# mLSTM head norm: the scale moved from VectorE into ScalarE's output gate

## The chip, the cores and the metric

The kernel runs on one core of a Trainium2 chip. The metric is the device time of the program in microseconds (us). TensorE is PE in the profile (PEld its weight loads), VectorE is DVE, ScalarE is ACT, GpSimd is POOL, SyncE is SP.

## The reference

One layer of a bidirectional encoder, in fp32, with D = 1024, on a prompt of 2048 positions and a sample of 256:

```python
def encoder_layer(x, ...):
    p = rmsnorm(x, norm1_w) @ w_in
    mq, mk, mv, mo, gates, aq, ak, av = split(p)
    m_out = mlstm_mixer(mq, mk, mv, mo, gates, b_gates, mh_norm_w)     # 8 heads of 64
    a_out = attention_mixer(aq, ak, av, q_norm_w, k_norm_w)            # 8 heads, 2 kv heads
    x = x + concatenate([m_out, a_out]) @ w_out
    u = centred_dwconv(rmsnorm(x, norm2_w) @ w_up, conv_w, conv_b)
    a, g = split(u)
    return x + (silu(g) * a) @ w_down                                  # then a final rmsnorm

def mlstm_mixer(...):
    ...
    h = h_f + h_b                                                      # forward and backward scans
    h = h * lax.rsqrt(jnp.mean(h * h, axis=-1, keepdims=True) + EPS)   # over the 64 of a head
    h = h * mh_norm_w
    return sigmoid(mo) * h
```

The change concerns the last three lines of `mlstm_mixer`.

## The kernel before

The 2304 tokens are worked as 18 tiles of 128 (NT) or 9 blocks of 256 (NB). fp32 products are made of three passes on a high and a low part of each operand ("split": ScalarE rounds, VectorE subtracts). The program has these stages, by the profile's clock: projections for attention and gates (to about 200 us); attention and mLSTM side by side (to 1450); the rest of attention beside phase_c, the output projection (to 1740); the rest of phase_c (to 1850); the up projection with its convolution; the down projection and the final norm.

`run_both` (L1562) steps two generators, `attention` (L458) and `mlstm` (L673), by estimated costs, and once the mLSTM is done it gives attention's steps out beside those of phase_c. The order that each engine runs is not this order of the code: the tile framework's scheduler puts the instructions of every engine in order from its own timeline of estimated costs, with priorities (`high_priority(offset=MPRI)` around the mLSTM's output steps). So a change of a few instructions can move many others.

The mLSTM works its 8 heads as 4 pairs, p = 0 to 3 (LASTP = 3). For each pair it has weights, projection (`proj`, `projT`), state updates (`upd`, `recur`), and then the output steps over the 18 tiles: `out_a` loads the decay matrix dm by a DMA of POOL's queue, masks it on POOL and takes Exp on ScalarE (L828), and for pairs 0 to 2 loads the gate tile `ogr` for two tiles of 128 (L833, POOL's queue); `out_b` and `out_c` make h; `out_d` follows DLAG = 6 steps later. The stored gate is the tanh form: sigmoid(mo) = 0.5 (1 + og), the half is in mhw.

In `out_c`, h is in the tile `hh` (128 tokens x 2 heads x 64) after L869. ScalarE squares each head with a sum along the row (L872), `rstd_of` makes r = (mean + eps)^-0.5 on POOL with two small operations (L97, L98), VectorE multiplies hh by r (L874) and, in pairs 0 to 2, makes (og + 1) * hh (L876). In `out_d` TensorE transposes hh (L881); pairs 0 to 2 scale it by mhw on ScalarE (L884); the last pair, whose gate is kept in transposed layout, multiplies by it on VectorE (L886). The result goes to mix_d in memory.

Attention takes scores (px, maximum over them on VectorE, L561), scores again with the maximum taken off (ps, L582 and L583), Exp on ScalarE (pe, L586), a rounded copy on ScalarE (xx, L587), the low part on VectorE (L588), and three products (pv, L599 to L601). At the end of a query block ScalarE copies the result out (L609), VectorE divides (L614, L615), and it goes to mix_d (L621).

phase_c (L945) takes for a block of 256 tokens eight chunks of mix_d (cmx: load L965, high part on ScalarE L966, low part on VectorE L967; chunk 7 is attention's last), 48 matmuls for each of four output slices z (`po`, L989), then adds the residual on VectorE (cx, L996, which frees the PSUM buffer), squares it on ScalarE (L999), sums (L1003), and at the end takes the norm (`rstd_bc`: PE L128, DVE L134, POOL L143 or, for the last block, ScalarE's square root and DVE L138 to L141, PE L145), and scales on VectorE (L1014). The blocks go in the order 0, 1, 2, 3, 4, 5, 8, 6, 7. In block 6, z = 0 and 1 are worked together and chunk 7 is taken last. Then the up projection loads and splits its first operands (n, rn, nt: L1077, L1092, L1096) and weights (L1110, L1125), and multiplies (pa, pb, pc at L1152).

Of the kernel before, what the change touches and what calls it, by code (L numbers as in the profile page):

```python
# [11 lines left out]
AF = mybir.ActivationFunctionType  # L12
ALU = mybir.AluOpType
# [4 lines left out]
P = 128  # L18
# [75 lines left out]
def rstd_of(g, pool, ms, n, name):  # L94
    nc = g.nc
    r = pool.tile([P, n], F32, tag="rstd", name=name)
    nc.gpsimd.tensor_scalar(r, ms, EPS, None, ALU.add)  # L97
    nc.gpsimd.tensor_tensor(r, r, g.mhalf[:, 0:n], ALU.pow)  # L98
    return r
# [573 lines left out]
def mlstm(g, tc, s1, sp, sw, sn, pj_, pm):  # L673


    nc = g.nc
# [177 lines left out]
    def out_c(s, i, o):  # L854
        nm = f"{s.p}_{i}"
        s1 = o.s1
        pN = pm.tile([P, 2, 2, 65], F32, tag="m", name="mN" + nm)
        for d in range(2):
            for h in range(2):
                nc.tensor.matmul(pN[:, d, h, :], o.dm[:, d, h, :], s.va[i // 2][:, i % 2, h, :], start=True, stop=True)  # L860
        nc.vector.tensor_tensor(s1, pN, s1, ALU.add)
        dn = sp.tile([P, 2, 2], F32, tag="dn", name="dn" + nm, bufs=4)
        nc.vector.scalar_tensor_tensor(dn, s1[:, :, :, 64], -1.0, s1[:, :, :, 64], ALU.mult, ALU.max)
        nc.vector.tensor_tensor(dn, dn, tm[:, i, 3, :, s.hs], ALU.max)
        nc.vector.reciprocal(dn, dn)
        nc.vector.tensor_tensor(s1[:, :, :, 0:64], s1[:, :, :, 0:64],
                                dn.unsqueeze(3).to_broadcast([P, 2, 2, 64]), ALU.mult)
        hh = o.hh = sp.tile([P, 2, 64], F32, tag="hh", name="hh" + nm, bufs=DLAG)
        nc.vector.tensor_tensor(hh, s1[:, 0, :, 0:64], s1[:, 1, :, 0:64], ALU.add)  # L869
        ms = sp.tile([P, 2], F32, tag="mms", name="mms" + nm, bufs=4)  # L870
        for h in range(2):
            nc.scalar.activation(s1[:, 0, h, 0:64], hh[:, h, :], AF.Square, scale=0.125, accum_out=ms[:, h:h + 1])  # L872
        r = rstd_of(g, sp, ms, 2, "mr" + nm)
        nc.vector.tensor_tensor(hh, hh, r.unsqueeze(2).to_broadcast([P, 2, 64]), ALU.mult)  # L874
        if s.p < LASTP:
            nc.vector.scalar_tensor_tensor(hh, o.og.rearrange("p (h d) -> p h d", h=2), 1.0, hh, ALU.add, ALU.mult)  # L876

    def out_d(s, i, o):
        nm = f"{s.p}_{i}"
# [25 lines left out]
    def out_steps(s):  # L905
        os_ = {}
        s.og = {}
        for i in range(NT + DLAG):
            if s.p == LASTP and i % 2 == 0 and i < NT:
                proj_qo(s, i // 2)  # L910
            if DLAG <= i:
                with tc.high_priority(offset=MPRI):
                    out_d(s, i - DLAG, os_.pop(i - DLAG))
            if 2 <= i < NT + 2:
                with tc.high_priority(offset=MPRI):
                    out_c(s, i - 2, os_[i - 2])
            if 1 <= i < NT + 1:
                with tc.high_priority(offset=MPRI):
                    out_b(s, i - 1, os_[i - 1])
            if i < NT:  # L920
                os_[i] = out_a(s, i)
            yield (2.7 if s.p < LASTP else OW3) if i < NT else 1
# [728 lines left out]
```

## Time and profile before

| | before |
|---|---|
| median of 3 runs | 3327.17 us (3326.01 to 3334.67) |
| profiled execution | 3327.39 us, span 3325.7 us |
| busy: PE, DVE, ACT, POOL | 97%, 73%, 60%, 16% |
| mean granted TensorE clock | 0.992 |

The times are of whole executions; the profile is of one further execution, its span is from the first to the last instruction. Lines such as L874 are those of the kernel before. In the changed kernel every line from L877 on has a number higher by 5, so L989 there is L994, and L996 there is L1001.

### The profile page before, as it was taken

How to read it: one execution, taken by the hardware profiler on the slowest of the kernel's cores; microseconds unless marked ns; L12 is line 12 of the kernel's file. 1: busy time of each engine (PE TensorE's matmuls, PEld its weight loads, DVE VectorE, ACT ScalarE, POOL GpSimd, SP SyncE). 2: the span in 40 equal slices, each digit the busy share in tenths (PEclk: the TensorE clock that was granted, in tenths of full speed). 3: DMA queues.
4: the chain of work that ended last, by engine and by line, in shares of the span. 5: the costliest groups of instructions: out<-in, count | busy, mean ns of one | idle time of the engine just before them, and what ended most of it. 6: DMA issues, size and time to landing. Idle time of an engine off the chain costs nothing.

```text
span 3325.7 us, 53327 instructions
## 1 busy us (share of the span) xinstructions
PE 3238.2 (97%) x19488; PEld 3017.3 (91%) x19488; DVE 2429.5 (73%) x3768; ACT 2002.8 (60%) x3765; POOL 519.0 (16%) x916
## 2 busy tenths in 40 slices
PE   8989999999999999999999899999999999999998
PEld 7878888888888878878889899999999999999998
DVE  7855676676657778786665899998888888666664
ACT  5646666666675676665552655666666667554543
POOL 4551033222232322210000000000000000010101
PEclk9999999999999999999999899999999999999999
DMA  9973333332335433533227666668676557967663
GB/s 348 319 207 108 113 113 102 110 108 94 109 114 177 131 110 120 162 100 107 85 89 266 230 240 211 231 231 273 205 266 235 202 199 252 318 229 269 216 238 127
DMA packets 364301, 612.31 MB, mean 184 GB/s; under 512 B 31605, under 2 KB 220455, under 8 KB 364039
## 3 DMA queue, kind: packets, MB, share of 16 engines
q1 hardware_dynamic: 330727, 563.14, 50.4%
q0 software_dynamic: 11856, 33.96, 3.7%
q10 hardware_dynamic: 21456, 11.80, 1.2%
q8 instruction: 154, 2.52, 0.3%
q14 instruction: 108, 0.88, 0.1%
HBM read 444.85 MB, written 163.93 MB: 183 GB/s over the span
## 4 chain that ended last, share of the span: by engine, by line
PE 58%; issue 3%; DVE 2%; DMA 2%; ACT 2%; POOL 1%; SPq 0%; POOLq 0%; DVEq 0%; ACTq 0%
PE pa L1152 17%; PE pc L1152 8%; PE pf L1416 7%; PE po L989 5%; PE pb L1152 4%; PE ph L1416 4%; PE pg L1416 2%; PE ps L582 1%; PE mj L745 1%; PE ps L583 1%; PE pv L599 1%; PE pv L601 1%; PE pv L600 1%; PE px L559 1%; PE mv L745 1%
## 5 line engine op out<-in xcount | busy, mean ns | idle before, releaser
L588 DVE TENSOR_TENSOR xx<-pe,xx 128x1024 fp32r<-128x1024 f32 x260 | 318.8, 1227 | 128.1 <-ACT xx L587 126.5
L561 DVE TENSOR_REDUCE mx<-px 128x1 f32<-128x1024 f32 x256 | 310.8, 1217 | 100.2 <-PE px L559 99.1
L586 ACT ACTIVATE pe<-ps 128x1024 f32<-128x1024 f32 x260 | 266.4, 1025 | 171.0 <-PE ps L583 164.2
L587 ACT ACTIVATE xx<-pe 128x1024 fp32r<-128x1024 f32 x260 | 274.9, 1058 | 5.0
L1369 POOL TENSOR_TENSOR sq<-sq,sq 128x384 f32<-128x384 f32 x38 | 48.8, 1284 | 1377.9 <-ACT sq L1365 1294.9
L989 PEld LDWEIGHTS po<-cmx,wo 128*128 128x128 f32 x1728 | 227.2, 189 | 17.9 <-DVE cx L996 1.2
L989 PE MATMUL po<-cmx,wo 128*128 128x256 f32 x1728 | 234.6, 283 | 1.2 <-DVE cx L996 0.8
L1156 ACT ACTIVATE u<-pa 128x386 f32<-128x386 f32 (+2 forms) x264 | 129.1, 489 | 175.4 <-PE pa L1152 169.4
L601 PE MATMUL pv<-xx,vv 128*128 128x512 f32 x520 | 210.8, 405 | 7.4 <-DVE xx L588 7.3
L599 PE MATMUL pv<-xx,vv 128*128 128x512 f32 x520 | 211.5, 407 | 6.5 <-ACT rs L609 3.2
L582 PE MATMUL ps<-qq,kk 128*128 128x512 f32 x520 | 213.3, 410 | 3.1 <-DVE mx L561 1.5
L583 PE MATMUL ps<-qm,kl 65*128 65x512 f32 x520 | 208.6, 401 | 0.0
L600 PE MATMUL pv<-xx,vl 128*64 128x512 f32 x520 | 206.9, 398 | 0.0
L717 PEld LDWEIGHTS mj<-mn,wm 128*128 128x128 f32 x1296 | 177.6, 192 | 18.4 <-ACT og L733 4.1
L717 PE MATMUL mj<-mn,wm 128*128 128x256 f32 x1296 | 190.2, 287 | 3.3 <-ACT og L733 2.9
L727 PE MATMUL mv<-wm,mn 128*128 128x256 f32 x1296 | 188.6, 286 | 1.3 <-ACT qb L723 1.3
L727 PEld LDWEIGHTS mv<-wm,mn 128*128 128x128 f32 x1296 | 174.6, 190 | 14.0 <-ACT qb L723 2.3
L238 PE MATMUL pj<-w_a,n1T 128*128 128x512 f32 (+1 forms) x864 | 168.5, 354 | 10.0 <-ACT w_a L105 7.1
L238 PEld LDWEIGHTS pj<-w_a,n1T 128*128 128x128 f32 x864 | 141.8, 192 | 29.8 <-ACT w_a L105 7.1
L559 PE MATMUL px<-kk,qq 128*128 128x512 f32 x512 | 165.6, 404 | 2.8 <-ACT pe L586 2.5
L828 ACT ACTIVATE dm<-dm,tm 128x128 f32<-128x128 f32 x288 | 95.6, 392 | 101.1 <-POOL dm L825 97.1
L1152 PE MATMUL pc<-nt,wb 128*128 128x386 f32 (+2 forms) x792 | 147.2, 340 | 0.3 <-DVE cx L1014 0.3
(336 smaller groups left out, 8114.8 us busy)
## 6 DMA issues: line engine op xcount, KB each, us to landing
mn<-n_d SPq DMA_DIRECT2D x216, 256.0 KB, 3.1
ru<-w_up SPq DMA_DIRECT2D x88, 512.0 KB, 5.7
rs<-wsu_d SPq DMA_DIRECT2D x88, 512.0 KB, 5.7
act_d<-ts SPq DMA_DIRECT2D x33, 768.0 KB, 6.1
nt<-act_d SPq DMA_DIRECT2D x60, 384.0 KB, 4.6
re_t<-wsd_d SPq DMA_DIRECT2D x45, 512.0 KB, 5.4
wsu_d<-tw SPq DMA_DIRECT2D x44, 512.0 KB, 4.1
act_d<-ya SPq DMA_DIRECT2D x99, 192.0 KB, 2.9
```

The costliest lines, as they stand in the source:

```text
L238: nc.tensor.matmul(pjs[t][:, c0:c1], nTs[tiles[t]][:, c, a, :], ws[c][:, b, c0:c1], start=(c == 0 and k == 0), stop=(c == NCC - 1 and k == 2))
L561: nc.vector.tensor_reduce(s.mx[:, t0, z0:z0 + 1], ps, AX.X, ALU.max)
L582: nc.tensor.matmul(o, kk[:, kc:kc + P], s.qq, start=True, stop=False)
L586: nc.scalar.activation(pe, ps, AF.Exp)
L587: nc.scalar.activation(x[:, 0], pe, AF.Copy)
L588: nc.vector.tensor_tensor(x[:, 1], pe, f32(x[:, 0]), ALU.subtract)
L599: nc.tensor.matmul(s.pv, vv[:, kt % 4, :], x1, start=kt == 0, stop=False)
L717: nc.tensor.matmul(pj[:, o].rearrange("p (n t) -> p n t", t=P), s.w[c][:, a, o * P:(o + 1) * P], nT[c][:, :, h, :], start=(c + o + k == 0) ...
L727: nc.tensor.matmul(pv[:, o], nT[c][:, o, a, :], s.w[c][:, h, 256:512], start=(c + o + k == 0), stop=(c == NCC - 1 and k == 2 and o == 1))
L989: nc.tensor.matmul(po[:, o], wo[c][z // 2][:, a, n], mx[c][:, h, :], start=c + o + k == 0, stop=c == NCC - 1 and o == 1 and k == 2)
L1152: s.nc.tensor.matmul(p, w[:, aa, c, :], ops[k][:, c, bb, 0:s.n], start=c == 0 and i == 0 and not add, stop=c == NCC // 2 - 1 and i == 2, s ...
L1416: nc.tensor.matmul(ps[c], w[:, aa, c, :], t[:, gi - g0, bb, 0:H], start=gi == 0 and m == 0 and not more, stop=gi == NG - 1 and m == 2, ski ...
```

## The change

```diff
@@ out_c
         r = rstd_of(g, sp, ms, 2, "mr" + nm)
-        nc.vector.tensor_tensor(hh, hh, r.unsqueeze(2).to_broadcast([P, 2, 64]), ALU.mult)
         if s.p < LASTP:
-            nc.vector.scalar_tensor_tensor(hh, o.og.rearrange("p (h d) -> p h d", h=2), 1.0, hh, ALU.add, ALU.mult)
+            og = o.og.rearrange("p (h d) -> p h d", h=2)
+            for h in range(2):
+                nc.scalar.activation(og[:, h], og[:, h], AF.Identity, scale=r[:, h:h + 1], bias=r[:, h:h + 1])
+            nc.vector.tensor_tensor(hh, og, hh, ALU.mult)
+        else:
+            for h in range(2):
+                nc.scalar.activation(hh[:, h], hh[:, h], AF.Copy, scale=r[:, h:h + 1])
```

VectorE's product by r (L874, 72 of them) goes. In pairs 0 to 2, ScalarE makes og * r + r in place, one activation per head (L877 after, 108), and VectorE multiplies that by hh (L878 after, 54). In the last pair ScalarE scales hh by r, one activation per head (L881 after, 36). ScalarE has 144 instructions more and VectorE 72 fewer; those of TensorE, POOL and SP are the same in number, and in another order from the first output tile on.

ScalarE at the first output tiles of pair 0 (s1 and hh belong to tile 0, 1, 2 by their second number; dm, pe, xx, qm are the decay matrix and attention's tiles), before:

```order
L872 ACTIVATE s10_0_4964,mms0_0_5021<-hh0_0_5019 128x64 x2
L828 ACTIVATE dm0_4_5156<-dm0_4_5156,tm_91 128x128 x4
L872 ACTIVATE s10_1_5036,mms0_1_5081<-hh0_1_5079 128x64 x2
L574 ACTIVATE qm0_4_4166<-pr0_4_4476 1x512
L586 ACTIVATE pe3_0_6_4487<-ps3_0_6_4482 128x1024
L587 ACTIVATE xx3_0_6_4488<-pe3_0_6_4487 128x1024
L872 ACTIVATE s10_2_5096,mms0_2_5139<-hh0_2_5137 128x64 x2
L828 ACTIVATE dm0_5_5412<-dm0_5_5412,tm_91 128x128 x4
```

The same place after the change:

```order
L872 ACTIVATE s10_0_4964,mms0_0_5021<-hh0_0_5019 128x64 x2
L877 ACTIVATE ogr0_0_4935<-ogr0_0_4935,mr0_0_5024 128x64 x2
L828 ACTIVATE dm0_4_5159<-dm0_4_5159,tm_91 128x128 x4
L872 ACTIVATE s10_1_5037,mms0_1_5082<-hh0_1_5080 128x64 x2
L877 ACTIVATE ogr0_0_4935<-ogr0_0_4935,mr0_1_5085 128x64 x2
L574 ACTIVATE qm0_4_4166<-pr0_4_4476 1x512
L586 ACTIVATE pe3_0_6_4487<-ps3_0_6_4482 128x1024
L587 ACTIVATE xx3_0_6_4488<-pe3_0_6_4487 128x1024
L872 ACTIVATE s10_2_5098,mms0_2_5141<-hh0_2_5139 128x64 x2
L828 ACTIVATE dm0_5_5416<-dm0_5_5416,tm_91 128x128 x4
L877 ACTIVATE ogr0_2_5051<-ogr0_2_5051,mr0_2_5144 128x64 x2
```

The scaling L877, which reads POOL's mr, stands directly behind the squares of its tile in tiles 0 and 1, and behind the next dm in tile 2.

TensorE where chunk 7 of block 6 is first needed (the second number in cmx6_7 is the chunk), before; the last pv stands 108 rows earlier:

```order
L989 MATMUL po6_1_20421<-cmx6_3_20070,wo3_0_17167 128x256 x3
L989 MATMUL po6_1_20421<-cmx6_4_20074,wo4_0_17193 128x256 x3
L989 MATMUL po6_1_20421<-cmx6_5_20078,wo5_0_17203 128x256 x3
L989 MATMUL po6_1_20421<-cmx6_6_20082,wo6_0_17249 128x256 x3
L989 MATMUL po6_0_20420<-cmx6_7_20380,wo7_0_17259 128x256 x6
L989 MATMUL po6_1_20421<-cmx6_7_20380,wo7_0_17259 128x256 x6
```

The same matmuls after the change, with the last pv, attention's last matmul:

```order
L601 MATMUL pv7_12_19789<-xx7_12_7_19983,vv1_16_12_10584 128x512
L994 MATMUL po6_1_20493<-cmx6_3_20142,wo3_0_17239 128x256 x2
L994 MATMUL po6_1_20493<-cmx6_4_20146,wo4_0_17265 128x256 x3
L994 MATMUL po6_1_20493<-cmx6_5_20150,wo5_0_17275 128x256 x3
L994 MATMUL po6_1_20493<-cmx6_6_20154,wo6_0_17321 128x256 x3
L128 MATMUL rs_c8_20591<-ones_84,cacc8_20238 128x2 x2
L145 MATMUL rs_c8_20591<-ident_73,rcol_c8_20594 128x128 x2
L994 MATMUL po6_0_20492<-cmx6_7_20452,wo7_0_17331 128x256
L994 MATMUL po6_1_20493<-cmx6_7_20452,wo7_0_17331 128x256
L994 MATMUL po6_0_20492<-cmx6_7_20452,wo7_0_17331 128x256 x5
L994 MATMUL po6_1_20493<-cmx6_7_20452,wo7_0_17331 128x256 x5
L994 MATMUL po6_2_20620<-cmx6_0_20130,wo0_1_17194 128x256 x3
```

Attention's last pv has come to stand 11 matmuls and the norm of block 8 ahead of the first use of chunk 7, where 314 matmuls stood between.

VectorE at that place, after the change (rn is an operand of the up projection, cmx6_7 the low part of chunk 7, cx6_0 the residual sum that frees a PSUM buffer):

```order
L972 TENSOR_TENSOR cmx6_7_20452<-cmx6_7_20452 128x256
L1101 TENSOR_TENSOR rn0_0_0_20183<-rn0_0_0_20183 128x386
L1101 TENSOR_TENSOR rn0_0_0_20183<-rn0_0_1_20185,rn0_0_0_20183 128x386
L1101 TENSOR_TENSOR rn0_0_1_20185<-rn0_0_1_20185,rn0_0_0_20183 128x386
L1001 TENSOR_TENSOR cx6_0_20456<-po6_0_20492,cx6_0_20456 128x512
L1101 TENSOR_TENSOR rn0_1_0_20242<-rn0_1_0_20242 128x386
```

and before, where other chunks' low parts stand there:

```order
L967 TENSOR_TENSOR cmx7_5_20412<-cmx7_5_20412 128x256
L967 TENSOR_TENSOR cmx7_6_20416<-cmx7_6_20416 128x256
L967 TENSOR_TENSOR cmx7_7_20656<-cmx7_7_20656 128x256
L996 TENSOR_TENSOR cx6_0_20384<-po6_0_20420,cx6_0_20384 128x512
L996 TENSOR_TENSOR cx6_1_20385<-po6_1_20421,cx6_1_20385 128x512
```

The sum cx6_0 has come to stand behind the three rn operations.

TensorE at the norm of the last block, after the change (pa and pb are the up projection's first tiles):

```order
L994 MATMUL po7_3_20922<-cmx7_7_20728,wo7_1_17332 128x256 x3
L1157 MATMUL pa_0_22_20980<-n11_0_20115,wa0_22_20977 128x386 x10
L1157 MATMUL pb_0_22_20993<-n21_0_20116,wa0_22_20977 128x386 x10
L1157 MATMUL pa_0_0_21025<-n11_0_20115,wa0_0_21022 128x386 x12
L1157 MATMUL pb_0_0_21038<-n21_0_20116,wa0_0_21022 128x386 x12
L128 MATMUL rs_c7_21071<-ones_84,cacc7_20810 128x2 x2
```

Before, L128 of rs_c7 stands directly behind the last matmul of po7_3:

```order
L989 MATMUL po7_3_20850<-cmx7_5_20412,wo5_1_17204 128x256 x3
L989 MATMUL po7_3_20850<-cmx7_6_20416,wo6_1_17250 128x256 x3
L989 MATMUL po7_3_20850<-cmx7_7_20656,wo7_1_17260 128x256 x3
L128 MATMUL rs_c7_20999<-ones_84,cacc7_20738 128x2 x2
L128 MATMUL rs_c7_20999<-ones_84,csq7_3_20901 128x2 x2
```

The 44 matmuls of L1157 have moved from ahead of block 7 to ahead of its norm.

## Prediction

> **What bounds the kernel now.** I read the page's table of busy times first, then its chain, then the waits of TensorE, and last the busy times by stage, cut where the mLSTM's output loop starts (420), where it has ended (1450), where attention ends (1735) and where the up projection has started (1850).
>
> ```profile
> PE 3238.2 (97%) x19488; PEld 3017.3 (91%) x19488; DVE 2429.5 (73%) x3768; ACT 2002.8 (60%) x3765; POOL 519.0 (16%) x916
> PE 58%; issue 3%; DVE 2%; DMA 2%; ACT 2%; POOL 1%; SPq 0%; POOLq 0%; DVEq 0%; ACTq 0%
> ```
>
> ```profile
> 420.00:1450.00 1030.00, 1000.56 (x6200) 865.95 (x6199) 732.08 (x1420) 690.30 (x1580) 295.40 (x584) 0.99 0.39 120
> 1450.00:1735.00 285.00, 282.35 (x1776) 246.99 (x1776) 192.89 (x272) 159.12 (x223) 10.95 (x19) 1.00 0.30 97
> 1735.00:1850.00 115.00, 97.41 (x760) 96.00 (x759) 73.49 (x135) 37.47 (x61) 3.15 (x5) 0.93 0.73 252
> 1850.00:3326.00 1476.00, 1461.26 (x8327) 1459.87 (x8325) 1157.80 (x1426) 875.34 (x1429) 55.88 (x47) 1.00 0.67 231
> ```
>
> The columns of the second fence are the stretch, its length, then the busy time (and instructions) of PE, weight loads, DVE, ACT and POOL, the granted clock, the DMA share and GB/s. TensorE sets the pace in every stage. In the stage that the change edits it is idle for 1030.00 - 1000.56 = 29.4 us, and no relief of VectorE can give more than that. DVE is busy for 71% of the stage, ACT for 67%: neither is full.
>
> ```profile
> PE rs_c L145 <- DVE rcol_c L141: 15.2, 1, 15.2
> PE pv L601 <- DVE xx L588: 7.3, 10, 1.4
> PE pv L599 <- ACT xx L587: 3.0, 5, 0.9
> PE px L559 <- ACT pe L586: 2.5, 3, 1.4
> PE rs_c L128 <- ACT csq L999: 1.2, 1, 1.2
> ACT pe L586 <- PE ps L583: 164.2, 136, 6.7
> DVE hh L874 <- POOL mr L98: 73.4, 46, 5.2
> ```
>
> These are waits: the waiter, whom it waited for, microseconds in total, times, the longest. No wait of TensorE names the mLSTM's output lines; what it loses to VectorE in that loop is little pieces behind attention's subtraction (7.3 us), and to ScalarE behind exp and copy (3.0 + 2.5). ScalarE mostly waits for TensorE in attention (164.2 us), so it has slack. VectorE stands 73.4 us at L874 until POOL has the rstd: that is the wait that the change takes from VectorE.
>
> **The change part by part.**
>
> ```profile
> L872 ACT ACTIVATE s<-hh x144: 237/243/283, 425.2 to 1439.3; 128x64 f32<-128x64 f32 x144
> L874 DVE TENSOR_TENSOR hh<-hh,mr x72: 275/292/712, 428.4 to 1442.3; 128x128 f32<-128x128 f32 x72
> L876 DVE SCALAR_TENSOR_TENSOR hh<-ogr,hh x54: 225/291/723, 429.3 to 1242.2; 128x128 f32<-128x128 f32 x54
> L805 ACT ACTIVATE C<-mu x128: 202/219/229, 247.0 to 1274.9; 64x65 f32<-64x65 f32 x128
> ```
>
> The durations are minimum/median/maximum in ns.
>
> *VectorE.* All 72 products of L874 go: 72 x 0.292 = 21.0 us of busy time. The 54 of L876 become plain products of the same shape; L874 is such a product and takes 0.292 against 0.291, so nothing. The 73.4 us of waits go too, since hh and the scaled gate now come to VectorE with other work in between. None of the 94 us is on TensorE's path as such; together they are an upper bound that the 29.4 us of idle TensorE cuts down.
>
> *ScalarE.* 144 new activations of 128x64. The nearest rows are L872, the same shape, and L805, another scaled copy of nearly that size: 144 x 0.219 = 31.5 to 144 x 0.243 = 35.0 us; I take 35.0. ACT goes from 690 to 725 us of 1030 in the stage, 70%. That is work beside TensorE's, covered by ACT's waits for L583. If that cover were gone, attention's exp would be late and px and pv after it.
> The Trainium skill speaks against the move: "ScalarE: Activation LUTs", Rules for kernel authors, tells authors to keep multiplications on VectorE, and budgets about 0.3 us per activation with a pointer operand plus 0.83 ns an element. By that an estimate is 144 x 0.353 = 51 us, 16 more than by L872's row; ACT would then be 72% busy, and my sum would be the same.
>
> *The wait on the rstd.* It does not vanish, it changes engine: ScalarE now needs r. In its new order ScalarE has nothing between the squares and the scaling in 7 of the 72 tiles, one instruction in 14, two to ten in the others. Behind a waiting ScalarE stand attention's exp and copy and the mLSTM's own Exp, for which VectorE and then TensorE wait. The bounds: all 73.4 us reach ScalarE (a loss), or the other work hides them (no loss). I weigh lost against won as equal here: ScalarE loses some of what it lost to TensorE anyway, VectorE brings attention's subtraction (L588) earlier. I put the stage at 0, with -15 and +18 as ends (worked out under the rivals).
>
> *The order of TensorE.* The scheduler deals out TensorE's work anew from the first output tile on. Three places matter.
>
> First, the end of attention. Before, 314 matmuls of phase c stood between attention's last matmul and the first that needs chunk 7 of block 6, the chunk which that attention block writes. After, 11 matmuls and the norm of block 8 stand there. The rows of before give the latency that this chunk needs, from the end of the last pv (1739.69 + 0.39 = 1740.1):
>
> ```profile
> 1739.69 0.39 PE L601 MATMUL pv<-xx,vv 128*128 128x512 f32 x1
> 1739.92 10.39 PE L989 MATMUL po<-cmx,wo 128*128 128x256 f32 x86
> 1741.32 0.38 ACT L609 ACTIVATE rs<-pv 64x256 f32<-64x256 f32 x1
> 1741.73 1.76 DVE L614 RECIPROCAL rs<-rs 128x128 f32<-128x128 f32 x2 [2.12 <-ACT rs L609]
> 1743.53 0.42 DVE L615 TENSOR_TENSOR o<-o,rs 128x256 f32<-128x256 f32 x1
> 1744.02 1.13 SPq L621 DMA_DIRECT2D mix_d<-o  x2
> mix_d<-o POOLq DMA_DIRECT2D x70, 64.0 KB, 2.6
> cmx<-mix_d SPq DMA_DIRECT2D x72, 128.0 KB, 2.5
> L966 ACT ACTIVATE cmx<-cmx x72: 399/417/421, 1406.9 to 1779.7; 128x256 fp32r<-128x256 f32 x72
> L967 DVE TENSOR_TENSOR cmx<-cmx x72: 405/415/427, 1409.0 to 1780.1; 128x256 fp32r<-128x256 f32 x72
> ```
>
> Counted from 1740.1, the two stores are issued at 3.9 and, half of the 1.13 later, 4.5 us; the second lands 2.6 later (7.1; POOL's row stands for SP's queue), the load of the chunk goes out then and lands 2.5 later (9.6), then L966 0.4 and L967 0.4: 10.4. TensorE has 11 x 0.121 = 1.3 us of matmuls (10.39 / 86 = 0.121 each) and 0.50 + 0.60 for the norm of block 8 (next fence): it stands for 10.4 - 2.4 = 8.0 us. Before, the same latency lay under 314 x 0.121 = 38 us.
>
> Second, right behind it: the 48 matmuls of po6_2 need a buffer that VectorE frees at L996, and L996 now stands behind three L1096 whose input loads (L1092) go out behind that cmx load.
>
> ```profile
> 1737.53 0.69 DVE L996 TENSOR_TENSOR cx<-po,cx 128x512 f32<-128x512 f32 x1 [1.45 <-PE po L989]
> 1748.45 0.90 SPq L1092 DMA_DIRECT2D rn<-n_d  x2
> 1750.14 0.50 PE L128 MATMUL rs_c<-ones,cacc 128*128 128x2 f32 x4
> 1752.31 0.56 DVE L1096 TENSOR_TENSOR rn<-rn 128x386 f32<-128x386 f32 x1 [0.86 <-DMA rn<-n_d]
> 1754.52 0.60 PE L145 MATMUL rs_c<-ident,rcol_c 128*128 128x128 f32 x4
> 1754.90 1.16 DVE L1096 TENSOR_TENSOR rn<-rn,rn 128x386 f32<-128x386 f32 x2 [1.37 <-DMA rn<-n_d]
> ```
>
> The second load was used 6.0 us after its issue (1748.45 and half of 0.90, to 1754.90). Both loads stand in SP's queue behind the chunk's, so the second is issued at about 7.9 and is there at 13.9; 1.16 and L996's 0.69 give 15.7. TensorE has done its 12 matmuls of the chunk at 10.4 + 1.4 = 11.8: 3.9 us more.
>
> Third, the norm of the last block, the 15.2 us wait. VectorE is the bound there: its queue of splits and of weights' products is full while TensorE stands.
>
> ```profile
> 1830.00:1845.00 15.00, 1.15 (x5) 1.15 (x6) 13.11 (x19) 10.33 (x13) 0.00 (x0) 0.50 1.03 372
> 1845.00:1850.00 5.00, 4.69 (x22) 4.39 (x21) 4.89 (x12) 2.40 (x5) 1.05 (x2) 0.79 0.06 23
> 1844.72 3.44 PE L1152 MATMUL pc<-nt,wb 128*128 128x386 f32 x12
> ```
>
> After, 44 matmuls of L1152 stand ahead of that norm which before ran earlier. At 1461.26 / 8327 = 0.175 each they cover 7.7 us: 7.5 are left of 15.2, and the 1.2 us wait of L128 is covered. VectorE's queue does not get shorter, so the cover gains no more than this.
>
> Idle time at the end, then: 8.0 + 3.9 + 7.5 = 19.4 against 15.2 + 1.2 = 16.4: +3.0.
>
> *Clock.* The granted clock was 0.50 while TensorE stood and 0.79 in the 5 us behind it; the 12 matmuls after the wait took 3.44 us, where 12 x 0.175 is 2.1. So a wait of several microseconds costs about 1.3 us more than its length. After there are three such waits for one: +1.3 to +2.6; I take +2, the 3.9 us one being short.
> "TensorE: Matmul & The Clock Gate", Part 1, in the Trainium skill says that an idle window of about 3.4 us halves the clock and that a busy one of that length frees it; by it, an estimate, a stall costs 1.7 us more than its length. The rows at 1830 and 1845 agree with the rule, and the sum by it, 2 x 1.7, would be 1.4 us higher.
>
> *Sum.* 0 (stage) + 3.0 + 2 = +5 us on the profiled execution's 3327.4 (span 3325.7 and 1.7 around it), which is 0.2 above the median of 3327.17: 3332. What a measurement of this kernel can tell from no change is 0.3%, 10 us, so the likeliest is no difference that can be told, on the slow side. Its own range is 3321 to 3338: the order of 420 to 1450 may give or take 7, the end 4.
>
> **Rivals.**
> *ScalarE becomes the one that is late.* L877 waits for POOL with exp behind it. VectorE's idle in the stage is 1030 - 732 = 298 us, 73.4 of it at L874; if the same 73.4 on ScalarE reach TensorE in the proportion in which all of VectorE's idle comes with TensorE's (29.4 of 298, a tenth), it is 7; if a quarter reaches, as where exp is the next in line, 18. With the end: 3339 to 3350. For it: 21 of the 72 tiles have at most one instruction between the squares and the scaling, and r takes L97 and L98. Against it: ScalarE's 164 us of waits for L583. It decides from about 5 us on. Chance 0.22.
>
> ```profile
> L97 POOL TENSOR_SCALAR mr<-mms x72: 217/221/1075, 425.9 to 1439.7; 128x2 f32<-128x2 f32 x72
> L98 POOL TENSOR_TENSOR mr<-mr,mhalf x72: 708/722/751, 426.8 to 1440.0; 128x2 f32<-128x2 f32 x72
> ```
>
> That is 0.22 + 0.72 us, which two or three of ScalarE's instructions cover: why I hold it to be less likely than the sum.
>
> *VectorE's relief frees TensorE* (the other side). With 94 us less of work and waits, VectorE no longer delays attention's subtraction (7.3 us) nor the mLSTM's chain, and half of the stage's 29.4 us goes: -15 + 5 = 3317; all of it, 3303. It decides from two thirds (20 us), or half where the end is cheaper. For it: DVE is the busier of the two engines in the stage. Against: TensorE's waits by name give VectorE only a third. Chance 0.16.
>
> *The end costs nothing.* If attention's stores and loads find other matmuls ready, or the shift of 314 matmuls also shortens attention's tail (at most 2.65 us idle from 1450 to 1735), the end gives 3 back through the third place: 3324. Chance 0.12, no measurable change.
>
> **How the numbers follow.** The sum 0.50, ScalarE late 0.22, relief 0.16, end free 0.12. Of the sum's 0.50, about 0.07 lies above 3337. Faster by over 0.3%: 0.15 (relief where it is over 10 us). Slower: 0.20 + 0.07 = 0.27. The same: 0.58. The range leaves out the outer ends of relief and of a late ScalarE: 3314 to 3346.
>
> **What would show it.** In the profile after: L874's 73.4 us gone from VectorE's waits, and a wait of ScalarE's L877 on POOL's L98 of 10 to 40 us. In the 1030 us of the stage TensorE still idle by 20 to 40. A wait of TensorE on cmx (L966 or L967 of before) of 6 to 9 us right after the last pv; one on cx L996 of 2 to 5; the wait on L141 down to 6 to 9 from 15.2. Wrong would be: a stage shorter by over 10 us, or ScalarE's wait above 60 us with TensorE waiting for exp, or no stall after attention.

## The result and the profile after

| | before | after |
|---|---|---|
| median of 6 runs | 3329.74 us (3326.01 to 3334.67) | 3340.53 us (3338.70 to 3341.63) |
| ratio | | 1.0029, 95% interval 1.0018 to 1.0039 |
| span of the profiled execution | 3325.7 us | 3337.8 us |
| forecast | | 3332 us, range 3314 to 3346 |

The three runs of before that the prediction had were joined by three more, so its median is now 3329.74. By the interval the change makes the kernel 6 to 13 us slower (10.8 by the medians), at the edge of the 0.3% that the prediction took as the least that can be told. The page's row of busy times looks much as before, with VectorE a little less busy and ScalarE a little more:

```profile
PE 3244.4 (97%) x19488; PEld 3018.2 (90%) x19488; DVE 2411.9 (72%) x3696; ACT 2042.4 (61%) x3909; POOL 518.7 (16%) x916
```

Since the two orders give the same matmuls in different places, equal stretches of the clock hold different work. So I cut both traces at the same events: the first square of the output loop, the mLSTM's last transpose, attention's last pv, and the first pc of the up projection. Busy times by these stages (stretch, length, then busy and instructions of PE, PEld, DVE, ACT, POOL, clock, DMA share, GB/s), before:

```profile
425.20:1443.97 1018.77, 990.05 (x6139) 857.25 (x6138) 721.53 (x1399) 683.16 (x1568) 292.05 (x577) 0.99 0.40 121
1443.97:1740.09 296.12, 292.74 (x1840) 255.78 (x1839) 201.31 (x281) 162.75 (x228) 11.17 (x19) 1.00 0.30 96
1740.09:1844.70 104.61, 87.33 (x706) 86.85 (x706) 66.13 (x120) 34.43 (x55) 2.10 (x3) 0.93 0.79 273
```

and after:

```profile
424.50:1417.57 993.07, 964.59 (x6026) 833.87 (x6025) 682.85 (x1304) 702.24 (x1685) 286.29 (x575) 0.99 0.40 123
1417.57:1782.29 364.72, 358.02 (x2264) 314.36 (x2263) 238.45 (x338) 192.05 (x274) 13.83 (x22) 0.99 0.29 93
1782.29:1858.10 75.81, 54.00 (x395) 52.62 (x394) 50.76 (x86) 25.65 (x36) 1.61 (x2) 0.88 0.86 303
```

From the first square to the first pc it takes 1419.5 us before and 1433.6 after, for the same matmuls (8682 and 8681 records). TensorE's idle time is length less busy: 28.7, 3.4 and 17.3 us before; 28.5, 6.7 and 21.8 after. The output loop, where the engines were exchanged, has the same idle time as before. Attention's tail lost 3.3, its end 4.5. The other 6.5 of the 14.1 us are a longer busy time for the same matmuls in these two executions; half of it goes with the clock, as shown further down. Behind pc the traces differ by 1.3 us the other way.

TensorE's waits from 1450 to 1865 us, after:

```profile
PE rs_c L145 <- DVE rcol_c L141: 8.8, 1, 8.8
PE po L994 <- DVE cx L1001: 5.9, 3, 4.6
PE po L994 <- ACT cmx L971: 4.9, 2, 4.0
PE ps L582 <- DVE mx L561: 2.8, 1, 2.8
PE rs_c L145 <- POOL rcol_c L143: 2.8, 1, 2.8
```

Where one wait of 15.2 us stood out before, the longest is now 8.8, and behind it stand several of 2.8 to 4.6. What happened around r in the loop, after (waiter, what it waited for; us, times):

```profile
L877 ACT ACTIVATE ogr<-ogr,mr x108: 424/436/468, 426.8 to 1226.2; 128x64 f32<-128x64 f32 x108
L881 ACT ACTIVATE hh<-hh,mr x36: 331/337/351, 1272.4 to 1415.1; 128x64 f32<-128x64 f32 x36
ACT ogr L877 <- POOL mr L98: 14.2, 21, 1.8
DVE hh L878 <- ACT ogr L877: 48.4, 32, 6.5
```

VectorE's 73.4 us of waits on POOL are gone. ScalarE waits 14.2 us in their place (2.5 more in the last pair), and VectorE 48.4 us for ScalarE's scaled gate. The loop's idle time of TensorE is as long as before, but it is not the same idle time. Some of its waits between 424 and 1445 us, four rows of before and then three of after:

```profile
PE pv L601 <- DVE xx L588: 5.7, 8, 1.4
PE pr L572 <- DVE m4r L569: 2.9, 1, 2.9
PE pv L599 <- ACT xx L587: 1.9, 3, 0.9
PE ps L582 <- ACT pe L586: 1.5, 3, 1.0
...
PE pv L599 <- ACT xx L587: 5.8, 8, 1.8
PE ps L582 <- ACT pe L586: 5.2, 6, 2.5
PE pv L601 <- DVE xx L588: 4.4, 5, 1.9
```

Added up from the loop's first square to its last transpose, TensorE waits for VectorE 12.7 us before and 4.7 after, and for ScalarE 15.3 before and 22.3 after.

### The profile page after: what moved, and what is told of

It reads as the page before. It is cut to its first block, busy times and chain, and to the rows that moved or that the text cites. A ratio compares the mean times of both kernels' runs of the same rounds, so it can differ in the third digit from the quotient of the medians.

```text
span 3337.8 us, 53366 instructions
## 1 busy us (share of the span) xinstructions
PE 3244.4 (97%) x19488; PEld 3018.2 (90%) x19488; DVE 2411.9 (72%) x3696; ACT 2042.4 (61%) x3909; POOL 518.7 (16%) x916
## 4 chain that ended last, share of the span: by engine, by line
PE 80%; issue 6%; DMA 4%; ACT 4%; DVE 3%; POOL 2%; SPq 0%; POOLq 0%; ACTq 0%; DVEq 0%
PE pa L1157 17%; PE pc L1157 8%; PE pf L1421 7%; PE po L994 6%; PE pb L1157 4%; PE pj L238 4%; PE mv L727 4%; PE ph L1421 3%; PE mj L717 3%; PE ps L582 3%; PE ps L583 3%; PE pv L599 3%; PE pv L601 3%; PE pv L600 3%; PE px L559 2%
## 5 line engine op out<-in xcount | busy, mean ns | idle before, releaser
L561 DVE TENSOR_REDUCE mx<-px 128x1 f32<-128x1024 f32 x256 | 310.6, 1217 | 96.7 <-PE px L559 95.7
L994 PE MATMUL po<-cmx,wo 128*128 128x256 f32 x1728 | 243.3, 285 | 11.3 <-DVE cx L1001 5.9
L717 PEld LDWEIGHTS mj<-mn,wm 128*128 128x128 f32 x1296 | 176.8, 191 | 17.3 <-ACT og L733 4.2
L1157 PE MATMUL pc<-nt,wb 128*128 128x386 f32 (+2 forms) x792 | 148.2, 341 | 0.0
```

Source lines behind the costliest of these rows:

```text
L561: nc.vector.tensor_reduce(s.mx[:, t0, z0:z0 + 1], ps, AX.X, ALU.max)
L717: nc.tensor.matmul(pj[:, o].rearrange("p (n t) -> p n t", t=P), s.w[c][:, a, o * P:(o + 1) * P], nT[c][:, :, h, :], start=(c + o + k == 0) ...
L994: nc.tensor.matmul(po[:, o], wo[c][z // 2][:, a, n], mx[c][:, h, :], start=c + o + k == 0, stop=c == NCC - 1 and o == 1 and k == 2)
L1157: s.nc.tensor.matmul(p, w[:, aa, c, :], ops[k][:, c, bb, 0:s.n], start=c == 0 and i == 0 and not add, stop=c == NCC // 2 - 1 and i == 2, s ...
```

## The experiments

All were timed against the kernel before on the same chip (medians 3331.6 to 3331.9 there). Two theories were set against each other. END: the order in which the scheduler put the work behind the mLSTM makes the loss. SWAP: the activations on ScalarE, and VectorE's new wait for them, make it in the loop.

**e1, the kernel before with an end like that of after.** No instruction changes engine. The order in the loop changes too (6034 matmuls stand in it, 6139 before).

```diff
-LEAD = 1.3
+LEAD = 1.45
```

> The instructions of the kernel before, with one number changed (LEAD 1.45 for 1.3, how far attention may lag behind the mLSTM when the code is written out): now 13 matmuls stand between attention's last one and the first that needs chunk 7 of block 6 (319 before, 16 after the change), and 45 ahead of the last block's norm (1 before, 45 after). No product has changed engine. Theory END (the loss comes from the order behind the mLSTM, not from the engines): 3337 to 3342 us, a stall of 6 to 11 us in TensorE behind the last pv, the wait on L141 down to about 9. Theory SWAP (ScalarE's 436 ns activations and VectorE's new wait for them cost TensorE the time): 3326 to 3331.

Measured: 1.0043 (1.0030 to 1.0055), 3344.0 us. The end by the same events, and its waits:

```profile
1780.89:1857.20 76.31, 54.01 (x394) 53.13 (x392) 50.83 (x86) 25.97 (x36) 1.40 (x2) 0.85 0.86 304
PE rs_c L145 <- DVE rcol_c L141: 8.8, 1, 8.8
PE po L989 <- ACT cmx L966: 8.0, 1, 8.0
PE po L989 <- DVE cx L996: 4.4, 2, 3.5
```

The end idles for 22.3 us against 21.8 after the change, while the loop's idle is 29.0. A loss as large as the change's is there without any exchange of engines. END holds. The 8.0 us behind cmx are the size of the prediction's first term.

**e2, after with 300 matmuls of cover.**

```diff
-CSTEPS = 52
+CSTEPS = 36
```

> The changed kernel with one number changed (CSTEPS 36 for 52, how many steps of phase c are written out beside attention's end): TensorE's order is the changed kernel's to 800 matmuls behind the mLSTM's last transpose, then 300 matmuls stand between attention's last one and chunk 7 of block 6, as in the kernel before, and 13 ahead of the last block's norm. Theory END: the 10 us come back, 3327 to 3333, no wait of TensorE on cmx or cx above 1 us and a wait on L141 of about 13. Theory SWAP: the stage of the output loop is the same, so 3337 to 3341.

Measured: 1.0094 (1.0081 to 1.0107), 3361.7 us: a miss for both theories. The loop is that of after (idle 27.8), the wait on cmx is gone, and in its place stands a longer one:

```profile
PE po L994 <- DVE cx L1001: 26.5, 2, 25.6
...
1762.73 0.43 DVE L972 TENSOR_TENSOR cmx<-cmx 128x256 fp32r<-128x256 f32 x1 [5.04 <-ACT cmx L971]
...
1769.52 4.02 DVE L1082 TENSOR_TENSOR n<-n 128x772 fp32r<-128x772 f32 x4
1777.98 0.56 DVE L1101 TENSOR_TENSOR rn<-rn 128x386 f32<-128x386 f32 x1 [4.45 <-DMA rn<-n_d]
1778.66 1.35 DVE L1001 TENSOR_TENSOR cx<-po,cx 128x512 f32<-128x512 f32 x2
```

The first row is TensorE's wait, the others are some of VectorE's in time. In this order VectorE takes the chunk (behind 5.0 us of waiting), the rn and the n operations, of which the last rn waits 4.5 us for its load, and only then the cx that would free a PSUM buffer. Cover on TensorE was worth nothing here, since the engine that must release it stood in its own queue. That is still an end effect, but "long cover, no loss" was too simple.

**e3, the third term alone.** The kernel before, `CSTEPS = 42`.

> The kernel before with CSTEPS 42: the same order of TensorE up to matmul 9900, 319 matmuls of cover as before, and 38 of the up projection's matmuls ahead of the last block's norm instead of 1. It tests the third term of the prediction alone: 38 x 0.175 = 6.7 us of the 15.2 us wait covered, so 8 to 9 us left and 3321 to 3325 us. If VectorE's queue gets longer by what those matmuls need, the wait stays above 13 and the time at 3327 to 3331. SWAP says nothing of it.

Measured: 1.0005 (0.9995 to 1.0014), no change: the wait came out as forecast, the gain of 6.7 us did not. The two longest waits of its end:

```profile
1778.80 14.06 PE L989 MATMUL po<-cmx,wo 128*128 128x256 f32 x96 [6.24 <-ACT cmx L966]
1848.57 1.22 PE L145 MATMUL rs_c<-ident,rcol_c 128*128 128x128 f32 x4 [9.50 <-DVE rcol_c L141]
...
1777.19 0.85 ACT L1076 ACTIVATE nt<-nt 128x772 fp32r<-128x772 f32 x1 [9.93 <-DMA nt<-n2t_d]
1778.29 0.42 ACT L966 ACTIVATE cmx<-cmx 128x256 fp32r<-128x256 f32 x1 [0.25 <-DMA cmx<-mix_d]
```

The wait on the norm fell to 9.5, near what was worked out, and 6.2 us came back earlier, as a wait for block 6's first chunks. The last two rows, ScalarE's, show why: the chunk stands behind an nt operation whose load ScalarE awaits for 9.9 us; its own load went out late too. Before, no nt stood ahead of block 6's first chunks. So the cover for the norm was paid for elsewhere.

**e4, only the last pair.** In pairs 0 to 2 L874 and L876 as before.

> Only the last pair's part of the change (36 activations on ScalarE for 18 products on VectorE); pairs 0 to 2 as before. TensorE's order is that of the kernel before up to matmul 7262 and the end has the cover of before (319, 1). END: 3326 to 3331, no difference. SWAP: a quarter of 10 us, 3331 to 3333, with VectorE or ScalarE later in the last pair's output loop.

Measured: 0.9995 (0.9987 to 1.0004). With the end's order kept, a quarter of the exchange costs nothing that can be told.

**e12, the exchange in pairs 0 to 2 with another end.** TensorE's order is that of after through these pairs.

```diff
-                nc.scalar.activation(hh[:, h], hh[:, h], AF.Copy, scale=r[:, h:h + 1])
+                nc.vector.tensor_scalar(hh[:, h], hh[:, h], r[:, h:h + 1], None, ALU.mult)
```

> The changed kernel with only the last pair's scaling taken back to VectorE (per head, 36 small operations); pairs 0 to 2 keep ScalarE's 108 activations, and TensorE's order is the changed kernel's up to matmul 7158, behind these pairs. The order that comes out has 122 matmuls (15 us) between attention's last one and chunk 7 of block 6, and VectorE takes the residual sums ahead of the rn operations. Theory END: the loss behind the mLSTM goes, no stall on cmx or cx above 1.5 us there: 3323 to 3331 us. Theory SWAP (ScalarE's activations in the loop cost the time): three quarters of the 10 us stay, 3337 to 3341.

Measured: 0.9992 (0.9983 to 1.0002), 3329.5 us. Its loop and its end:

```profile
427.60:1439.07 1011.47, 983.37 (x6073) 847.71 (x6072) 699.57 (x1352) 703.53 (x1659) 289.16 (x577) 0.99 0.40 121
1773.39:1854.50 81.11, 66.03 (x507) 65.65 (x505) 56.19 (x96) 28.86 (x44) 2.31 (x2) 0.91 0.84 300
```

Three quarters of ScalarE's new work are there, the loop's idle is 28.1, and the loss is gone; the end idles 15.1 us, 6.7 less than after, attention's tail 3.9, 2.8 less. A wait on cx of 6.2 us that I had not expected stands there too, so the end is better, not free. SWAP as the cause of the loss falls, with e4 for the last pair. (The traced execution of e12 took 3335.8 us, 6.3 above its median, so its busy time is not compared.)

**e10 and e11, rn on POOL.** To take the second stall by itself; e11 is the same edit on the kernel before.

```diff
-            todo = [lambda c=c: n2_sums(g, s1, 0, c) for c in range(NCC // 2)]
+            todo = [lambda c=c: n2_sums(g, s1, 0, c, ('gpsimd',) * 4) for c in range(NCC // 2)]
```

> The changed kernel with the subtractions of the up projection's first operands (rn, L1101, 16 of them in this stage) on POOL, which is idle there: TensorE's order stays, cx6_0 to cx6_3 no longer stand behind rn on VectorE. It tests the second stall by itself. END with VectorE's queue as cause: the waits of TensorE on cx (5.9 us) fall below 1.5, the wait on cmx stays at 4 and that on the power at 3; 3333 to 3337. If the loads and not VectorE's order hold cx back, or POOL is late for the last norm, 3339 to 3345.

> The same edit on the kernel before, whose cx does not stand behind rn: the control. No wait on cx is there to be taken away, so 3324 to 3331, unless VectorE's relief of 16 x 0.55 = 9 us ahead of the last norm shortens its wait of 15.2: then 3318 to 3323.

Measured: e10 1.0034 (1.0021 to 1.0046), e11 1.0005 (0.9996 to 1.0014). Nothing came of it. TensorE's waits on cx fell from 5.9 us to 5.4, where below 1.5 was forecast if VectorE's queue is the cause; e11 shows no difference either. With rn off VectorE in e10, the residual sums still come late:

```profile
PE po L994 <- DVE cx L1001: 5.4, 2, 4.0
1811.83 1.42 DVE L1001 TENSOR_TENSOR cx<-po,cx 128x512 f32<-128x512 f32 x2 [5.62 <-DMA cx<-xT]
```

VectorE waits there for the load of cx itself, which SP issues at 1805.7 us (L982). After the change it waits 7.1 us at the same place for a load of rn, and then another 0.2 for that of cx. Both loads come late; taking rn away does not remove the second stall.

The other five ask where the product by r would best stand.

**e5, the same arithmetic on VectorE.** In after, both activations become `nc.vector.tensor_scalar` with r as pointer operand.

> The changed kernel's arithmetic (og * r + r per head, then one product; in the last pair hh * r per head) with VectorE in ScalarE's place: 144 small operations more on VectorE than after the change, none on ScalarE, and VectorE waits for POOL's r again. In the order that comes out, 132 matmuls (16 us) stand between attention's last one and chunk 7 of block 6, and 49 ahead of the last block's norm. Theory END (the order behind the mLSTM makes the time, the engines in the loop do not): 3326 to 3335 us, no wait on cmx after the last pv, the output loop's TensorE idle 26 to 32 us. Theory RELIEF (VectorE's work and wait in the loop cost TensorE time, ScalarE's do not): slower than after the change, above 3341, and the loop's idle above 35.

Measured: 0.9964 (0.9952 to 0.9977), 3320.1 us, faster than both kernels.

**e6, no product by r at all.**

> The product by r is left out on every engine (the heads are not normalized; squares and POOL's power stay), VectorE makes (og + 1) * hh alone: nobody waits for r. It bounds what any placing of this product can bring in the output loop. 116 matmuls of cover behind attention, 49 ahead of the last norm. END and the prediction's zero for the loop: TensorE idle in the loop 25 to 30 us, as with either engine, 3322 to 3333. RELIEF: the loop's idle falls by a third or more, below 20, and 3312 to 3320.

Measured: 0.9946 (0.9933 to 0.9958), 3313.5 us. The loops of e5 and e6:

```profile
424.20:1425.37 1001.17, 979.19 (x6106) 844.59 (x6104) 727.83 (x1465) 672.88 (x1556) 293.29 (x577) 1.00 0.40 123
426.40:1420.27 993.87, 977.96 (x6108) 844.52 (x6107) 696.93 (x1320) 670.94 (x1554) 288.85 (x575) 1.00 0.41 123
```

TensorE idles 22.0 us in the loop of e5 and 15.9 in that of e6, against 28.7 before. So without the product TensorE idles 13 us less in the loop, though VectorE still waits 39.3 us there, for ScalarE's squares (L872), which read hh before it is written again. How much of the 13 is the product with its wait and how much the order that came out is not shown. END predicted 26 to 32 and 25 to 30 for these loops: wrong for both.

**e13, e14, e15: hh scaled per head on ScalarE, the same on VectorE, and the gate scaled on POOL.** e13 and e14 are the kernel before with two operations for L874 (nothing worked into the gate); e15 is after with `nc.gpsimd.tensor_scalar` for both activations.

> The kernel before with hh * r made by ScalarE per head in all four pairs (144 activations with one pointer operand), and (og + 1) * hh on VectorE as before: no working of the scale into the gate. Cover 103 matmuls, 49 ahead of the last norm. If ScalarE as the place of the scaling is what keeps the loop's idle of TensorE at the 28 us of before and after (against 22 with VectorE's small operations): idle 27 to 31 and 3326 to 3334 us. If the working into the gate is what costs or brings something, the idle differs from after by over 4 us.

> The kernel before with L874's product written as two operations per tile with r as a pointer operand, on VectorE, in all pairs; nothing worked into the gate. 72 more operations on VectorE. Cover 103, 49 ahead of the last norm. If the gain of the run with the scale on VectorE (3320 us, loop idle 22) came from its order and not from the algebra, this one gives the same: idle 20 to 25 and 3318 to 3326. If it came from the algebra (only one product of hh behind r), the idle is 27 to 31 as before and the time 3324 to 3332 by the end alone.

> The changed kernel's arithmetic with the scaling of gate and last pair's hh on POOL, which makes r itself, so no other engine waits for r ahead of the scaling. Cover 125, 49 ahead of the last norm. If the place of the scaling matters through ScalarE's and VectorE's waits: loop idle of TensorE between 16 (no scale at all) and 24, 3313 to 3324. If POOL's operations are so slow that the decay mask (L825) for ScalarE's L828 comes late: idle above 28 and 3326 to 3340.

Measured: e13 1.0010 (1.0001 to 1.0019); e14 0.9979 (0.9970 to 0.9988); e15 0.9990 (0.9981 to 0.9999). Their loops:

```profile
424.20:1436.47 1012.27, 980.70 (x6073) 845.25 (x6072) 692.91 (x1316) 702.93 (x1695) 294.67 (x577) 0.99 0.40 121
425.90:1429.97 1004.07, 977.08 (x6072) 843.82 (x6071) 716.65 (x1460) 669.71 (x1551) 292.44 (x577) 0.99 0.40 122
424.40:1431.27 1006.87, 979.57 (x6080) 846.14 (x6080) 697.00 (x1317) 667.86 (x1552) 362.14 (x721) 0.99 0.40 122
```

The loop's idle is 31.6, 27.0 and 27.3 us. Between e13 and e14 only the engine of the product differs, and what the scheduler makes of it: ScalarE's idles 4.6 us more and the whole is 0.3% slower. Against e14, e5's working into the gate idles 5.0 less. POOL scales a gate in 0.393 us, and VectorE waits 65.6 us for it (L878): the wait has only changed engine again. e13 came out just beyond the idle of 27 to 31 us that was forecast, e14 at the lower end of the forecast for the algebra, e15 between its two forecasts for the idle.

## Why the prediction came out as it did

The direction, the place and the range were right. The median lies 8.5 us above the point: 2.6 of that is the median of before, which the three further runs raised, and the change costs 10.8 us where the sum has 5. Idle time of TensorE makes 7.6 us in the two traces (loop -0.2, attention's tail 3.3, end 4.5) where the sum has 3.0; that leaves 3.2 of the 10.8 for the clock and all else, where the sum has 2. The largest miss is attention's tail. Step by step:

- *The loop at zero.* Confirmed: idle 28.5 against 28.7, and as lost against won, which the prediction weighed as equal: TensorE waits 8.0 us less for VectorE and 7.0 more for ScalarE. Kernels that share the order of before up to their end have 11.6 to 14.5 and 14.8 to 15.4 us of these two waits (e3, e4 but for its last pair, e11), those with the loop of after 3.5 to 4.5 and 21.6 to 23.1 (e2, e10). e1, with another order in the loop and no exchange, has 12.5 and 15.2. So both rivals came, the relief at about half of its 15 us, the late ScalarE at the lower end of its 7 to 18. That they cancel so nearly is luck: the prediction had no working for it and gave -15 and +18 as ends.
- *ScalarE's work.* 39.6 us more of busy time from the first square to pc (880.3 to 919.9), against 35.0 taken and 51 by the estimate from the Trainium skill's "ScalarE: Activation LUTs", Rules for kernel authors. By what ScalarE became busier the trace lies nearer to the row. By the activations alone it lies at the estimate: the 144 cover 41.8 + 10.5 = 52.3 us, and one L877 takes 0.436 us, more than that rule's 0.353. The difference is overlap, since an activation starts before the one ahead of it has ended (two L877 in a row take 0.78).
- *The end.* TensorE's rows behind the last pv (which ends at 1782.3), after, with the idle time ahead of each and its releaser:

```profile
1786.75 0.71 PE L145 MATMUL rs_c<-ident,rcol_c 128*128 128x128 f32 x4 [2.84 <-POOL rcol_c L143]
1791.48 2.96 PE L994 MATMUL po<-cmx,wo 128*128 128x256 f32 x12 [4.02 <-ACT cmx L971]
1795.35 11.68 PE L994 MATMUL po<-cmx,wo 128*128 128x256 f32 x96 [0.92 <-DVE cx L1001]
1811.59 7.49 PE L994 MATMUL po<-cmx,wo 128*128 128x256 f32 x48 [4.56 <-DVE cx L1001]
```

- *The first term, 8.0 us.* The chunk was ready 9.2 us after the last pv (10.4 worked out); TensorE stood 2.8 + 4.0 = 6.9 us, the norm's wait on POOL (L143) being the first part of it.
- *The second term, 3.9 us.* The buffer that I named cost 0.9. A wait of 4.6 stood one buffer later, on cx6_2, where VectorE waited for late loads of rn and of cx, and e10 shows that the load of cx is enough. The two add up to 5.5; that this is near 3.9 is chance.
- *The third term, 7.5 left.* 8.8 measured; e3 has 9.5.
- *Idle at the end.* +4.5 us measured against +3.0. Attention's tail, which the sum leaves out without a reason, added 3.3, most of it one wait on the maximum (2.8 us, L561).
- *The clock, +2.* Too small, but by how much stays open. In the two traces TensorE's busy time for the same matmuls is 6.5 us longer. Three of the seven stretches at half clock from the first square to pc, after:

```profile
1409.24:1416.07 6.83, 6.29 (x17) 4.47 (x17) 5.06 (x12) 4.89 (x12) 1.21 (x2) 0.50 0.18 53
1624.28:1627.70 3.42, 3.39 (x8) 2.62 (x9) 2.57 (x3) 1.08 (x2) 1.09 (x2) 0.50 0.42 115
1812.01:1815.43 3.42, 3.42 (x18) 3.42 (x17) 3.25 (x7) 0.90 (x3) 0.00 (x0) 0.50 1.02 384
```

Added up over all such stretches, TensorE was busy at half clock for 23.7 us from the first square to pc, and 16.7 before. At half clock work takes about twice as long (the 12 matmuls at 1791.48 above took 0.247 us each, against the prediction's 0.121), so half of the difference, 3.5 us, is lost to it. By stages it is 9.7 us in the loop after and 15.8 before, 6.8 and none in attention's tail, 7.2 and 0.9 at the end: half of the end's difference, 3.2 us, stands against the +2. That these stretches last 3.4 us or a multiple agrees with "TensorE: Matmul & The Clock Gate", Part 1, of the Trainium skill; they follow waits of under 3 us too, as at 1624 behind 2.8. The other 3 us of the 6.5 are not explained. Nor is the 6.5 shown to be the change's: kernels that share the order of before up to its end differ as much among themselves, 1370.1 to 1376.6 us of busy time for these matmuls (before, e3, e4, e11).

What stays open is why e5's loop idles 5 us less than e14's: whether the single product behind the scaled gate or only the order that came out. No run held the order fixed, and this holds for e6 as well.

## What to carry to other kernels

Where a scheduler deals out the order, cost a change in two parts: the engines' work where it stands, and the order of everything behind it; here the second made the loss (e1, e12). Look on the engine that releases TensorE for what stands ahead of the release in its queue: cover on TensorE did not help where a load was awaited there (e2, e3). Cut both traces at the same events and compare idle and busy separately, since equal clock times hold different work. A product that only moves to another engine takes its wait along: look for who waits for the new producer, and try the same algebra on the old engine first (e5: 0.36% faster than before).

## What the runs showed of the hardware

- An activation of 128x64 took 0.243 us with a constant scale (L872, a square), 0.337 with a scale taken from a tile (L881 after, a copy), and 0.436 with scale and bias from a tile (L877 after). On VectorE the operation of L877 in e5 took 0.312, or 0.249 with one such operand (L881 there), on POOL 0.393 (e15).

```profile
L877 DVE TENSOR_SCALAR ogr<-ogr,mr x108: 238/312/658, 427.4 to 1224.2; 128x64 f32<-128x64 f32 x108
L881 DVE TENSOR_SCALAR hh<-hh,mr x36: 242/249/451, 1274.0 to 1424.6; 128x64 f32<-128x64 f32 x36
L877 POOL TENSOR_SCALAR ogr<-ogr,mr x108: 383/393/1677, 426.8 to 1217.5; 128x64 f32<-128x64 f32 x108
```

The first two rows are of e5, the third of e15.

- In attention's tail a wait of 2.8 us, which ended at 1622.05, was followed by a stretch at a granted clock of 0.50, from 1624.28 to 1627.70.
